# A linear layer with a low-rank update: semaphores of its own, a looped program for TensorE, and x rounded to bf16 ahead of the transposes

## Chip, core and metric

One core of one Trainium2 chip. The metric is the device time of one execution in microseconds. The core's engines are TensorE (PE; its weight loads are listed as PEld), VectorE (DVE), ScalarE (ACT), GpSimd (POOL) and SyncE (SP), and 16 DMA engines move data between DRAM and the on-chip memory SBUF. Matmuls write to a second on-chip memory, PSUM. The engines run their own instruction streams and wait for each other with semaphores.

## What is computed

```python
# x: (16, 2048, 256), W: (256, 256), lora_A: (256, 16), lora_B: (16, 256), lora_E: (16,)
x_flat = x.reshape(-1, in_dim)                  # 32768 rows of 256
y = x_flat @ W
lora_out = x_flat @ lora_A
lora_out = lora_out * lora_E
lora_out = lora_out @ lora_B
y = y + scale * lora_out
return y.reshape(batch, seq_len, out_dim).astype(np.float32)
```

x and the output are 33.5 MB each, in fp32.

## The kernel before

The low-rank update is folded into the weights once: `weff = W + (A * E * scale) @ B`, kept in bf16 (lines 87 to 105). Each row of x then meets one product, `x @ weff`.

x is worked through in nine chunks, `PLAN` on line 11: 16 rows of all 128 partitions (2 MB), seven times 32 rows (4 MB), and 16 again. A partition's rows are contiguous in DRAM, so a 4 MB chunk is one run of 32 KB per partition. Six buffers `xy` (`SLOTS`) hold chunks; the result is written over the chunk's own x, and stored from there.

All large transfers are issued by the sync engine on one queue, in this order: W; loads of chunks 0 to 3 (`LEAD`); then, for each chunk i, its store (line 70) and the load of chunk i + 4 (line 66). From chunk 6 on, a load first waits until the store that last used its buffer has landed. ScalarE's queue issues the three small loads.

Inside a chunk the work goes by groups of two rows (`CG`). For a group TensorE transposes four 128x128 blocks of x in fp32 against an identity (line 113) into a PSUM tile, VectorE copies them to SBUF as bf16 (line 119), TensorE multiplies with `weff` (line 131, four matmuls with 256 columns), and ScalarE copies the fp32 result from PSUM into the chunk's buffer (line 139). TensorE runs one group ahead: the transposes of group n + 1 come before the products of group n. There are 128 groups; every instruction of every engine is written out, with no loop in the program. The order is the one in which the kernel is written, and the framework (`tc.manual_schedule()`) places the semaphores and the waits.

Of the kernel before, what the change touches and what calls it, by code (L numbers as in the profile page):

```python
# [1 line left out]

# [5 lines left out]

PLAN = [16] + [32] * 7 + [16]

ROWS, SLOTS = 32, 6

LEAD = 4
CG = 2


@with_exitstack
def kernel(  # L20
    ctx: ExitStack,
    tc: tile.TileContext,
    x: bass.AP,
    W: bass.AP,
    lora_A: bass.AP,
    lora_B: bass.AP,
    lora_E: bass.AP,
    scale: bass.AP,
    out: bass.AP,
):  # L30
    nc = tc.nc
    P = 128
    FP32 = mybir.dt.float32
    BF16 = mybir.dt.bfloat16

    x_flat = x.flatten_outer_dims()
    out_flat = out.flatten_outer_dims()
    N, K = x_flat.shape
    M = out_flat.shape[1]
    R = lora_B.shape[0]  # L40
    KC = K // P
    assert K == M and sum(PLAN) * P == N

    const = ctx.enter_context(tc.tile_pool(name="const", bufs=1))
    slots = ctx.enter_context(tc.tile_pool(name="slots", bufs=SLOTS))
    xTpool = ctx.enter_context(tc.tile_pool(name="xTpool", bufs=4))
    ps_setup = ctx.enter_context(tc.tile_pool(name="ps_setup", bufs=1, space=bass.MemoryType.PSUM))
    ps_xT = ctx.enter_context(tc.tile_pool(name="ps_xT", bufs=3, space=bass.MemoryType.PSUM))
    ps_y = ctx.enter_context(tc.tile_pool(name="ps_y", bufs=3, space=bass.MemoryType.PSUM))


    ctx.enter_context(tc.manual_schedule())

    starts = [sum(PLAN[:i]) * P for i in range(len(PLAN))]

    def rows_of(flat, i):
        b, r0 = PLAN[i], starts[i]
        return flat[r0:r0 + b * P, :].rearrange("(p b) k -> p b k", b=b)

    held = []

    def load(i):
        t = slots.tile([P, ROWS, K], FP32, name="xy")
        nc.sync.dma_start(out=t[:, :PLAN[i], :], in_=rows_of(x_flat, i))  # L66
        held.append(t)

    def store(i):
        nc.sync.dma_start(out=rows_of(out_flat, i), in_=held[i][:, :PLAN[i], :])  # L70

    w_sb = const.tile([P, KC, M], FP32)
    nc.sync.dma_start(out=w_sb, in_=W.rearrange("(c p) m -> p c m", p=P))  # L73
    a_sb = const.tile([P, KC, R], FP32)
    nc.scalar.dma_start(out=a_sb, in_=lora_A.rearrange("(c p) r -> p c r", p=P))
    b_sb = const.tile([R, M], FP32)
    nc.scalar.dma_start(out=b_sb, in_=lora_B)
    e_sb = const.tile([R, 1], FP32)
    nc.scalar.dma_start(out=e_sb, in_=lora_E[:, None])

    for i in range(LEAD):
        load(i)

    ident = const.tile([P, P], FP32)
    make_identity(nc, ident)

    b_bf = const.tile([R, M], BF16)
    nc.vector.tensor_copy(out=b_bf, in_=b_sb)  # L88
    ps_at = ps_setup.tile([R, KC, P], FP32, name="ps_at")
    for c in range(KC):  # L90
        nc.tensor.transpose(ps_at[:, c, :], a_sb[:, c, :], ident)  # L91
    ate = const.tile([R, KC, P], BF16)
    nc.vector.tensor_scalar(  # L93
        out=ate,
        in0=ps_at,
        scalar1=e_sb,
        scalar2=float(scale),
        op0=mybir.AluOpType.mult,
        op1=mybir.AluOpType.mult,
    )  # L100
    ps_aeb = ps_setup.tile([P, KC, M], FP32, name="ps_aeb")
    for c in range(KC):
        nc.tensor.matmul(ps_aeb[:, c, :], ate[:, c, :], b_bf, start=True, stop=True)  # L103
    weff = const.tile([P, KC, M], BF16)
    nc.vector.tensor_add(out=weff, in0=w_sb, in1=ps_aeb)  # L105

    groups = [(i, g) for i, b in enumerate(PLAN) for g in range(b // CG)]

    def transposed(i, g):
        psum_xt = ps_xT.tile([P, CG, KC, P], FP32, name="psum_xt")  # L110
        for j in range(CG):
            for c in range(KC):
                nc.tensor.transpose(  # L113
                    psum_xt[:, j, c, :],
                    held[i][:, g * CG + j, c * P:(c + 1) * P],
                    ident,
                )
        xt = xTpool.tile([P, CG, KC, P], BF16, name="xt")
        nc.vector.tensor_copy(out=xt, in_=psum_xt)  # L119
        return xt  # L120


    ready = transposed(*groups[0])
    for n, (i, g) in enumerate(groups):
        xt = ready
        if n + 1 < len(groups):
            ready = transposed(*groups[n + 1])
        psum_y = ps_y.tile([P, CG, M], FP32, name="psum_y")
        for j in range(CG):
            for c in range(KC):  # L130
                nc.tensor.matmul(  # L131
                    psum_y[:, j, :],
                    xt[:, j, c, :],
                    weff[:, c, :],
                    start=(c == 0),
                    stop=(c == KC - 1),
                )

        nc.scalar.copy(out=held[i][:, g * CG:(g + 1) * CG, :], in_=psum_y)  # L139
        if (g + 1) * CG == PLAN[i]:  # L140
            store(i)
            if i + LEAD < len(PLAN):
                load(i + LEAD)


# [1 line left out]
_INS = ['x', 'W', 'lora_A', 'lora_B', 'lora_E', 'scale']  # L147
_OUTS = [((16, 2048, 256), 'float32')]

_NUMBERS = {'scale': 1.0}  # L150


# [26 lines left out]
```

## Time and profile before

| | |
|---|---|
| three runs | 165.45, 166.19, 166.29 us; median 166.19 |
| profiled execution | 166.25 us, span 164.4 us |
| TensorE busy (matmul) | 123.3 us, 1028 instructions |
| TensorE weight loads | 102.9 us, 1028 instructions |
| VectorE busy | 90.0 us, 131 instructions |
| ScalarE busy | 76.3 us, 129 instructions |
| DMA | 67.56 MB, mean 411 GB/s over the span |
| first load issued | 1.22 us after the span's start |
| ScalarE's last copy begins | 138.1 us |

The span runs from the first to the last instruction of the profiled execution. A row of a group in the profile is: line, engine, operation, output and inputs by the program's names, shapes, count; then busy time and the mean duration of one in ns; then the idle time of the engine just before them, with what ended it. In the slices each digit is the busy share, in tenths, of one fortieth of the span. A row of windows has the stretch, its length, the busy time of each engine with the number of instructions (PE, PEld, DVE, ACT, POOL), TensorE's granted clock, the DMA engines' share and GB/s. A row of the chain or of issues begins with the start and the duration in us. A row of waits has who waited for whom, the sum, the number of times and the longest.

### The profile page before, as it was taken

How to read it: one execution, taken by the hardware profiler on the slowest of the kernel's cores; microseconds unless marked ns; L12 is line 12 of the kernel's file. 1: busy time of each engine (PE TensorE's matmuls, PEld its weight loads, DVE VectorE, ACT ScalarE, POOL GpSimd, SP SyncE). 2: the span in 40 equal slices, each digit the busy share in tenths (PEclk: the TensorE clock that was granted, in tenths of full speed). 3: DMA queues.
4: the chain of work that ended last, by engine and by line, in shares of the span. 5: the costliest groups of instructions: out<-in, count | busy, mean ns of one | idle time of the engine just before them, and what ended most of it. 6: DMA issues, size and time to landing. Idle time of an engine off the chain costs nothing.

```text
span 164.4 us, 2548 instructions
## 1 busy us (share of the span) xinstructions
PE 123.3 (75%) x1028; PEld 102.9 (63%) x1028; DVE 90.0 (55%) x131; ACT 76.3 (46%) x129; POOL 0.7 (0%) x6
## 2 busy tenths in 40 slices
PE   0179899999999999999999689992999995000000
PEld 0058788888888888888888478881888783000000
DVE  0065677777777777777777536771777673000000
ACT  0034566666666666666666525662566565000000
POOL 1000000000000000000000000000000000000000
PEclk9999999999999999999999978999999999655555
DMA  5999999998999999999999999999999999999991
GB/s 141 429 482 407 415 478 395 454 415 343 437 462 407 421 446 431 435 431 423 439 419 439 423 423 443 409 439 447 423 391 466 415 443 423 423 454 415 415 391 56
DMA packets 3211, 67.56 MB, mean 411 GB/s; under 512 B 624, under 2 KB 896, under 8 KB 896
## 3 DMA queue, kind: packets, MB, share of 16 engines
q1 hardware_dynamic: 2864, 67.37, 96.2%
q8 instruction: 8, 0.13, 0.3%
q10 hardware_dynamic: 336, 0.03, 0.2%
q14 instruction: 3, 0.02, 0.0%
HBM read 33.85 MB, written 33.55 MB: 410 GB/s over the span
## 4 chain that ended last, share of the span: by engine, by line
DMA 59%; PE 23%; ACT 1%; SPq 1%; DVE 0%; issue 0%
DMA xy<-in_x_dram 38%; DMA out_dram<-xy 21%; PE psum_y L131 12%; PE psum_xt L113 11%; ACT xy L139 1%; DVE xt L119 0%; SPq L66 0%; SPq L73 0%
## 5 line engine op out<-in xcount | busy, mean ns | idle before, releaser
L119 DVE CAST xt<-psum_xt 128x512 bf16<-128x512 f32 x128 | 88.5, 691 | 38.6 <-PE psum_xt L113 38.6
L139 ACT COPY xy<-psum_y 128x512 f32<-128x512 f32 x128 | 75.0, 586 | 52.7 <-PE psum_y L131 52.7
L113 PE MATMUL psum_xt<-ident,xy 128*128 128x128 f32 x512 | 79.2, 279 | 6.1 <-DMA xy<-in_x_dram 6.0
L131 PE MATMUL psum_y<-weff,xt 128*128 128x256 bf16 x512 | 79.3, 278 | 0.3 <-DVE xt L119 0.3
L113 PEld LDWEIGHTS psum_xt<-ident,xy 128*128 128x128 f32 x512 | 61.9, 144 | 9.2 <-issue 5.7
L131 PEld LDWEIGHTS <-xt 128*128 128x128 bf16 x512 | 41.1, 99 | 16.8 <-DVE xt L119 0.9
L139 ACT ACT_TABLE_LOAD x1 | 1.3, 1283 | 9.7 <-DMA xy<-in_x_dram 9.7
L103 PE MATMUL ps_aeb<-b_bf,ate 16*128 16x256 bf16 x2 | 0.6, 402 | 4.4 <-DVE ate L93 4.4
L91 PE MATMUL ps_at<-ident,a_sb 128*16 128x128 f32 x2 | 0.6, 396 | 4.0 <-DMA a_sb<-in_lora_A_dram 4.0
L88 DVE CAST b_bf<-b_sb 16x256 bf16<-16x256 f32 x1 | 0.3, 281 | 6.0 <-DMA b_sb<-in_lora_B_dram 6.0
L103 PEld LDWEIGHTS <-ate 16*128 16x128 bf16 x2 | 0.1, 102 | 4.9 <-DVE ate L93 4.9
L91 PEld LDWEIGHTS ps_at<-ident,a_sb 128*16 128x16 f32 x2 | 0.1, 88 | 4.0 <-issue 4.0
L93 DVE TENSOR_SCALAR ate<-ps_at,e_sb 16x256 bf16<-16x256 f32 x1 | 0.5, 472 | 2.2 <-DMA e_sb<-in_lora_E_dram 2.2
L105 DVE TENSOR_TENSOR weff<-w_sb,ps_aeb 128x512 bf16<-128x512 f32 x1 | 0.7, 689 | 0.7 <-PE ps_aeb L103 0.7
masks.py:199 POOL TENSOR_SCALAR_AFFINE_SELECT ident<-ident 128x128 f32<-128x128 f32 x1 | 0.3, 292 | 0.1
masks.py:197 POOL MEMSET ident<- 128x128 f32 x1 | 0.2, 204 | 0.3 <-POOLq L160 0.3
L160 POOL MEMSET const-bfloat16-1.0<- 128x1 bf16 x1 | 0.1, 101 | 0.0
L160 POOL MEMSET const-uint8-127<- 128x1 uint8 x1 | 0.1, 101 | 0.0
L160 POOL MEMSET const-float32-0.0<- 128x1 f32 x1 | 0.1, 98 | 0.2 <-issue 0.2
L160 POOL MEMSET const-float32-1.0<- 128x1 f32 x1 | 0.1, 98 | 0.0
## 6 DMA issues: line engine op xcount, KB each, us to landing
xy<-in_x_dram SPq DMA_DIRECT2D x7, 4096.0 KB, 38.0
out_dram<-xy SPq DMA_DIRECT2D x7, 4096.0 KB, 34.2
xy<-in_x_dram SPq DMA_DIRECT2D x2, 2048.0 KB, 26.6
out_dram<-xy SPq DMA_DIRECT2D x2, 2048.0 KB, 24.5
w_sb<-in_W_dram SPq DMA_DIRECT2D x1, 256.0 KB, 3.0
a_sb<-in_lora_A_dram ACTq DMA_DIRECT2D x1, 16.0 KB, 3.2
b_sb<-in_lora_B_dram ACTq DMA_DIRECT2D x1, 16.0 KB, 4.7
e_sb<-in_lora_E_dram ACTq DMA_DIRECT2D x1, 0.1 KB, 6.6
```

The lines of the kernel that those rows point to most:

```text
L88: nc.vector.tensor_copy(out=b_bf, in_=b_sb)
L91: nc.tensor.transpose(ps_at[:, c, :], a_sb[:, c, :], ident)
L93: nc.vector.tensor_scalar(out=ate, in0=ps_at, scalar1=e_sb, scalar2=float(scale), op0=mybir.AluOpType.mult, op1=mybir.AluOpType.mult,)
L103: nc.tensor.matmul(ps_aeb[:, c, :], ate[:, c, :], b_bf, start=True, stop=True)
L105: nc.vector.tensor_add(out=weff, in0=w_sb, in1=ps_aeb)
L113: nc.tensor.transpose(psum_xt[:, j, c, :], held[i][:, g * CG + j, c * P:(c + 1) * P], ident,)
L119: nc.vector.tensor_copy(out=xt, in_=psum_xt)
L131: nc.tensor.matmul(psum_y[:, j, :], xt[:, j, c, :], weff[:, c, :], start=(c == 0), stop=(c == KC - 1),)
L139: nc.scalar.copy(out=held[i][:, g * CG:(g + 1) * CG, :], in_=psum_y)
L160: nc = _bacc.Bacc("TRN2", target_bir_lowering=False, num_devices=1)
```

## The change

The same arithmetic by other means, with every large transfer at the same place in the sync engine's program.

- The tile framework's pools are gone; buffers are allocated by hand. The whole kernel is one critical section of the framework (`tc.tile_critical`), with its own semaphores for loads, stores and each hand-over. The section is opened and closed by the sync engine: when it is entered the sync engine issues a token and every engine waits for it; at its end the sync engine waits for all stores and for tokens of all engines.
- The unit of work is a step of four rows (`Q`), 64 of them. VectorE rounds four rows of x to bf16 into one of two buffers `xb` (`round_step`), TensorE transposes eight blocks of bf16 into one of two bf16 PSUM tiles, VectorE copies these to one of two `xt`, TensorE runs eight products into one of two PSUM tiles, and ScalarE copies the result of four rows at once.
- TensorE's operands are now the same in every second step, so that its program is a loop of 31 iterations with two steps each. Its semaphores are counted down as they are taken (`take`), so that the waits in the loop are constants too. The other engines' programs are written out.
- ScalarE drains before it signals that a chunk is ready for its store.

The core of the diff:

```diff
-CG = 2
+Q = 4
...
-    ctx.enter_context(tc.manual_schedule())
+    xy = [sbuf(f"xy{s}", [P, ROWS, K], FP32) for s in range(SLOTS)]
+    xb = [sbuf(f"xb{s}", [P, Q, K], BF16) for s in range(2)]
+    xt = [sbuf(f"xt{s}", [P, Q, KC, P], BF16) for s in range(2)]
...
+    ps_xt = [psum(f"ps_xt{s}", [P, Q, KC, P], BF16) for s in range(2)]
+    ps_y = [psum(f"ps_y{s}", [P, Q, M], FP32) for s in range(2)]
...
+    with tc.tile_critical(sync_engine=mybir.EngineType.SP, no_gpsimd_drain=True):
...
+        sp.dma_start(out=w_sb[:], in_=W.rearrange("(c p) m -> p c m", p=P)).then_inc(s_w, 16)
+        for i in range(LEAD):
+            load(i)
+        for i in range(CHUNKS):
+            sp.wait_ge(s_rdy, i + 1)
+            sp.dma_start(out=rows_of(out_flat, i), in_=xy[i % SLOTS][:, :PLAN[i], :]).then_inc(s_out[i], 16)
+            if i + LEAD < CHUNKS:
+                if i + LEAD >= SLOTS:
+                    sp.wait_ge(s_out[i + LEAD - SLOTS], 16)
                 load(i + LEAD)
+        for i in range(CHUNKS):
+            sp.wait_ge(s_out[i], 16)
...
+        def round_step(k):
+            i, r = steps[k]
+            if r == 0:
+                dve.wait_ge(s_in[i], 16)
+            if k >= 2:
+                dve.wait_ge(s_t, k - 1)
+            dve.tensor_copy(out=xb[k % 2][:], in_=xy[i % SLOTS][:, r:r + Q, :]).then_inc(s_xb, 1)
+
+        round_step(0)
+        for k in range(n):
+            if k + 1 < n:
+                round_step(k + 1)
+            dve.wait_ge(s_t, k + 1)
+            if k >= 2:
+                dve.wait_ge(s_p, k - 1)
+            dve.tensor_copy(out=xt[k % 2][:], in_=ps_xt[k % 2][:]).then_inc(s_xt, 1)
...
+        for k, (i, r) in enumerate(steps):
+            act.wait_ge(s_p, k + 1)
+            act.copy(out=xy[i % SLOTS][:, r:r + Q, :], in_=ps_y[k % 2][:]).then_inc(s_y, 1)
+            if r + Q == PLAN[i]:
+                act.drain().then_inc(s_rdy, 1)
...
+        def take(s):
+            pe.wait_ge(s, 1).then_inc(s, -1)
+
+        def transposes(k):
+            take(s_xb)
+            for j in range(Q):
+                for c in range(KC):
+                    t = pe.transpose(ps_xt[k % 2][:, j, c, :], xb[k % 2][:, j, c * P:(c + 1) * P], ident_bf[:])
+            t.then_inc(s_t, 1)
+
+        def products(k):
+            take(s_xt)
+            take(s_y)
+            for j in range(Q):
+                for c in range(KC):
+                    m = pe.matmul(
+                        ps_y[k % 2][:, j, :], xt[k % 2][:, j, c, :], weff[:, c, :],
+                        start=(c == 0), stop=(c == KC - 1),
+                    )
+            m.then_inc(s_p, 1)
...
+        transposes(0)
+        pe.wait_ge(s_lora, 4)
+        with pe.Fori(0, n // 2 - 1):
+            transposes(1)
+            products(0)
+            transposes(0)
+            products(1)
+        transposes(1)
+        products(0)
+        products(1)
```

The setup has the same products and one more cast, of the identity to bf16 (`ident_bf`), on VectorE.

## The prediction

> **What bounds the kernel now.** I read the page's slices first, then the windows from 2 us to 160 us and from there to the end, the chain of waits, the sync engine's own issues, and the groups by line last.
>
> ```profile
> PE   0179899999999999999999689992999995000000
> DMA  5999999998999999999999999999999999999991
> 2.00:160.00 158.00, 123.29 (x1028) 102.91 (x1028) 89.95 (x131) 76.25 (x129) 0.00 (x0) 0.93 1.00 426
> 160.00:164.40 4.40, 0.00 (x0) 0.00 (x0) 0.00 (x0) 0.00 (x0) 0.00 (x0) 0.50 0.14 60
> q1 hardware_dynamic: 2864, 67.37, 96.2%
> q8 instruction: 8, 0.13, 0.3%
> ```
>
> The 16 DMA engines have a share of 1.00 over 158 us, at 426 GB/s; 158 x 426 = 67.3 MB, which is all that the kernel moves. TensorE is done at slice 34 of 40 and the DMA goes on without it. Queue q8 is no data: eight packets that fetch instructions.
>
> ```profile
> 1.72 17.63 DMA xy<-in_x_dram
> 50.54 34.17 DMA out_dram<-xy
> 84.77 44.76 DMA xy<-in_x_dram
> 138.10 0.58 ACT xy L139
> ...
> 96.98 42.06 SPq L70 DMA_DIRECT2D out_dram<-xy  x4
> ...
> out_dram<-xy SPq DMA_DIRECT2D x2, 2048.0 KB, 24.5
> ```
>
> In the chain a 4 MB load that is issued at 84.77 lands 44.76 us later, though 4.19 MB at 426 GB/s is 9.8 us: the queue holds some 35 us of work ahead of it. The last result is written at 138.68, its 2 MB store is issued at 138.7, and it lands 24.4 us later, at 163.1; the work of its own is 4.9 us. So compute has slack, and the time is the bytes by the rate, plus 2 us of start and what stands behind the last landing. The span is 164.4, the profiled execution 166.25 (1.85 lie around the span); the median of the runs is 166.19, 0.06 lower.
>
> **How much slack.** A step is 4 rows of all 128 partitions; there are 64, eight in a large chunk and four in the first and last. Today TensorE sets its pace: four matmuls of a group take 0.44 to 0.52 us in the chain, a step has four such groups, 1.92 us. Let a step take p. Chunk 1 lands at 19.4 and everything behind it can run without a wait. With 2 us from the last product to the store's issue, chunk 7's store goes out at 21.3 + 56p. If the queue has run dry by then, 9.9 us for this store, 4.9 for the last and 2.4 of fixed latency follow (the 0.26 MB load of W, 0.6 us of bytes, took 3.0). 21.3 + 56p + 17.2 = 163.1 gives p = 2.22. The same sum for chunk 6 gives 2.4. Up to 2.2 us a step, compute moves nothing; the order in which the sync queue issues loads and stores, and the landing that each late load waits for (six slots), are the same in both programs.
>
> **The change part by part.**
>
> ```profile
> L119 DVE CAST xt<-psum_xt 128x512 bf16<-128x512 f32 x128 | 88.5, 691 | 38.6 <-PE psum_xt L113 38.6
> L139 ACT COPY xy<-psum_y 128x512 f32<-128x512 f32 x128 | 75.0, 586 | 52.7 <-PE psum_y L131 52.7
> L113 PE MATMUL psum_xt<-ident,xy 128*128 128x128 f32 x512 | 79.2, 279 | 6.1 <-DMA xy<-in_x_dram 6.0
> L131 PE MATMUL psum_y<-weff,xt 128*128 128x256 bf16 x512 | 79.3, 278 | 0.3 <-DVE xt L119 0.3
> L88 DVE CAST b_bf<-b_sb 16x256 bf16<-16x256 f32 x1 | 0.3, 281 | 6.0 <-DMA b_sb<-in_lora_B_dram 6.0
> SPq L160 <- PEq L160: 0.7, 1, 0.7
> SPq L174 <- PEq L174: 0.6, 2, 0.4
> ```
>
> *VectorE.* Added: 64 roundings of 1024 elements, SBUF to SBUF. The nearest row is the cast of 256 at line 88, 281 ns. [...] Moved: 128 copies of 512 become 64 of 1024, from bf16 in PSUM. [...] A step is 0.69 + 1.23 = 1.92, with two waits some 2.0 (1.4 to 2.5).
>
> [...]
>
> *ScalarE.* 64 copies of 1024: the 586 ns are 427 at 1.2 elements a ns and 159 fixed, so 0.85 + 0.16 = 1.01 us, and a drain a chunk; below VectorE.
>
> *TensorE.* Eight products keep 0.88 to 1.04 a step. Eight transposes of bf16 cost between a half and all of today's 0.88. Three semaphores are taken a step and a branch closes every two: 1.3 to 2.0 with 0.1 for these, and I take 1.6. VectorE is the slowest at 2.0, so compute ends a few us later than now, under 20 us of stores: nothing. If that cover went, each 0.1 us in a step would cost 56 x 0.1 = 5.6 us.
>
> *Start.* The section opens with a token from the sync engine that all wait for, ahead of W's load and the first load. Today's opening wait of this kind is 0.7 us, the two of line 174 0.3 each. The sync engine gives the token itself: +0.2 (0 to 0.7), and all of it is on the path, since every byte starts later. The other edits of the setup (one more cast, the identity in bf16) end before the first load lands or sit in the slack.
>
> *End.* After the last landing the sync engine passes nine waits, eight of them long met, then waits for all engines' tokens and gives one, before the closing that exists now: +0.3 (0 to 0.7, the same rows).
>
> *Instruction fetch.* TensorE's 2056 recorded instructions become a loop of some 70 with its waits. q8's 131 KB by 2056 is 64 bytes each, so q8 is this program; the eight packets go. Each holds one DMA engine for 0.3% x 16 x 164.4 / 8 = 1.0 us, and the trace has the data packet behind it late by some 0.45 more. As a mean over 16 engines that is 8 x 1.0 / 16 = 0.5; on the engine that ends last between 0 and 1.4. I take -0.5.
>
> *Semaphores of its own.* The waits of the loads and stores stand at the same places. Nothing.
>
> Sum on 166.25: +0.2 +0.3 -0.5 = 0, less the 0.06 to the median: 166.2 us. With all bounds 164.8 to 167.6.
>
> **The rivals.** *The fetches were worth more.* The last DMA engine ends over 1 us behind the next by the trace's packets, and if fetches made it the last, their full 1.4 goes and the tokens cost nothing: 166.2 - 1.4 = 164.8. For it: a packet of q8 lies in the last 30 us, when nothing evens it out. Against: data packets also show stretches in which one engine is some 5% slow, with no fetch near.
>
> *The tokens at their upper bounds*, with the fetches worth nothing: 166.2 + 1.4 = 167.6. For it: the opening wait of 0.7. Against: the two of 0.3.
>
> [...]
>
> *The loop does not hold its program* (slower, and the change would not do what it says): each of 31 backward branches waits for a packet of 16 KB, 1.0 us and the 2.4 of latency, 1.7 us a step on TensorE: p = 1.6 + 1.7 = 3.3, 21.3 + 56 x 3.3 + 17.2 = 223, and 226 in time. Against: two steps are well under the 256 instructions of one fetched packet. [...]
>
> **How the numbers follow.** What a measurement here can tell from no change is about 0.5%, 0.83 us. The forecast, within that of 166.2: 0.64. More from the fetches: 0.15. Tokens dear: 0.10. VectorE bound: 0.07. Refetching loop: 0.04. So faster 0.15, same 0.64, slower 0.21. The range runs from 164.9 to 167.7: it takes in the bounds of the tokens and fetches and leaves out the two compute cases, 0.11 together, and a little at the low end.
>
> **What would show it.** In the changed profile: DMA share still 1.00 from 2 us to 160 and 426 GB/s; q8 gone; the first load issued at 1.2 to 1.9; the rounding near 690 ns and the copy at 691 or 1225; ScalarE's last copy between 130 and 145 us, well before the last landing at 163; 1.3 to 2.0 from there to the end of the span. I am wrong if the DMA's slices fall under 9 ahead of the end, if the chain has VectorE or TensorE in its last 30 us, or if the rate of the full stretch is another than 426.

## The result and the profile after

| | before | after |
|---|---|---|
| 16 runs each | 166.14 us (165.45 to 166.64) | 167.18 us (166.42 to 167.74) |
| profiled execution | 166.25 us, span 164.4 | 166.75 us, span 165.0 |
| 27 and 10 runs on another occasion | 166.00 us | 166.85 us |

The changed kernel takes 1.0066 of the time before (95% interval 1.0054 to 1.0079), and 1.0047 (1.0030 to 1.0063) the second time: slower by some 0.8 to 1.0 us, about the 0.5% that was called the limit of what can be told. The forecast was 166.2 with a range from 164.9 to 167.7.

The page of the changed kernel, slices and groups:

```profile
PE   0159499999996599408994099902998591000000
DMA  5999998997999999999999999999999999999970
...
q1 hardware_dynamic: 2864, 67.37, 95.7%
...
q14 instruction: 3, 0.02, 0.0%
...
L160 ACT COPY xy<-ps_y 128x1024 f32<-128x1024 f32 x64 | 64.8, 1012 | 69.2 <-PE ps_y L181 69.2
L181 PE MATMUL ps_y<-weff,xt 128*128 128x256 bf16 x512 | 72.1, 288 | 0.8 <-PEq L167 0.3
L173 PE MATMUL ps_xt<-ident_bf,xb 128*128 128x128 bf16 x512 | 43.6, 235 | 30.4 <-PEq L167 30.4
L143 DVE CAST xb<-xy 128x1024 bf16<-128x1024 f32 x64 | 43.7, 684 | 32.9 <-DMA xy<-in_x_dram 32.9
L152 DVE COPY xt<-ps_xt 128x1024 bf16<-128x1024 bf16 x64 | 44.2, 690 | 10.2 <-PE ps_xt L173 9.1
```

TensorE now has holes of whole slices (VectorE waits 32.9 us in all for loads, TensorE 30.4 us ahead of its transposes), and the DMA is as full as it was: 1.00 and 426 GB/s from 2 us to 160. Queue q8, the fetches of TensorE's program, is gone from the list. A rounding takes 684 ns; the copy from PSUM has twice the elements of the old one and takes the same 690 ns. Behind a landed load the timeline has a step every 1.32 us, with TensorE back to back:

```profile
61.09 0.61 PE L173 MATMUL ps_xt<-ident_bf,xb 128*128 128x128 bf16 x8
...
62.41 0.61 PE L173 MATMUL ps_xt<-ident_bf,xb 128*128 128x128 bf16 x8
```

In the kernel before, the chain has 16 such steps from 20.12 to 49.45, 1.83 us each.

The two ends of the kernel before, first from the timeline of the sync engine (start and duration in us):

```profile
0.74 0.42 SPq L73 DMA_DIRECT2D w_sb<-in_W_dram  x1
1.22 1.90 SPq L66 DMA_DIRECT2D xy<-in_x_dram  x4
```

and then from the view of its closing line (least, median and largest duration in ns, first and last start in us):

```profile
L174 POOLq EVENT_SEMAPHORE_RANGE_CLEAR  x1: 96/96/96, 164.0 to 164.0; - x1
```

The same timeline of the changed kernel:

```profile
0.94 0.44 SPq L101 DMA_DIRECT2D w_sb<-in_W_dram  x1
1.44 1.89 SPq L99 DMA_DIRECT2D xy<-in_x_dram  x4
```

the view of the line that opens and closes its section:

```profile
L94 SPq NOP  x2: 13/13/13, 0.7 to 164.0; - x2
```

and that of its last line:

```profile
L237 POOLq EVENT_SEMAPHORE_RANGE_CLEAR  x1: 243/243/243, 164.4 to 164.4; - x1
```

The first load is issued 0.22 us later: the section's token stands before it (the first NOP, at 0.7), and after it a branch of every engine into the section (at 0.8). At the end the trace's semaphore events put the last wait for a store at 163.46 before and 163.48 after; from there to the span's end it is 0.94 us before and 1.49 after. Of the 0.55 more, 0.37 lie in the section's closing, a branch and the tokens (the second NOP, at 164.0, stands ahead of the framework's own closing), and 0.18 mostly in the clearing of the semaphores, 243 ns for 96. So 0.77 us are fixed costs at the two ends. The last store lands at the same time as before, though it started later: 163.08 against 163.11. In this pair of profiles, then, at most some 0.25 us were gained on the way.

Where the gain from the missing fetches went is seen in windows over the last 6 us (length; busy time by engine; TensorE's clock, the DMA share and GB/s last), before, after, and for the changed kernel with the loop written out (e7 below):

```profile
158.00:160.00 2.00, 0.00 (x0) 0.00 (x0) 0.00 (x0) 0.00 (x0) 0.00 (x0) 0.50 0.96 410
160.00:162.00 2.00, 0.00 (x0) 0.00 (x0) 0.00 (x0) 0.00 (x0) 0.00 (x0) 0.50 0.29 123
162.00:164.00 2.00, 0.00 (x0) 0.00 (x0) 0.00 (x0) 0.00 (x0) 0.00 (x0) 0.50 0.02 8
```

```profile
158.00:160.00 2.00, 0.00 (x0) 0.00 (x0) 0.00 (x0) 0.00 (x0) 0.00 (x0) 0.50 0.77 328
160.00:162.00 2.00, 0.00 (x0) 0.00 (x0) 0.00 (x0) 0.00 (x0) 0.00 (x0) 0.50 0.17 74
162.00:164.00 2.00, 0.00 (x0) 0.00 (x0) 0.00 (x0) 0.00 (x0) 0.00 (x0) 0.50 0.02 8
```

```profile
158.00:160.00 2.00, 0.00 (x0) 0.00 (x0) 0.00 (x0) 0.00 (x0) 0.00 (x0) 0.50 0.86 369
160.00:162.00 2.00, 0.00 (x0) 0.00 (x0) 0.00 (x0) 0.00 (x0) 0.00 (x0) 0.50 0.35 147
```

The share falls earlier after the change (0.77 and 0.17 for 0.96 and 0.29): most of the 16 engines are done sooner. From 162 to 164 us it is 0.02 both times (8 GB/s, one packet of 16 KB), and that packet belongs to the engine that ends last. The end is this engine's, and in this pair it did not move.

### The profile page after: what moved, and what is told of

Its sections match the earlier page's. It is cut to its first block, busy times and chain, and to the rows that moved or that the text cites. A ratio compares the mean times of both kernels' runs of the same rounds, so it can differ in the third digit from the quotient of the medians.

```text
span 165.0 us, 2679 instructions
## 1 busy us (share of the span) xinstructions
PE 97.6 (59%) x1028; PEld 85.6 (52%) x1028; DVE 84.0 (51%) x132; ACT 66.1 (40%) x65; POOL 0.7 (0%) x6
## 5 line engine op out<-in xcount | busy, mean ns | idle before, releaser
L160 ACT COPY xy<-ps_y 128x1024 f32<-128x1024 f32 x64 | 64.8, 1012 | 69.2 <-PE ps_y L181 69.2
L181 PE MATMUL ps_y<-weff,xt 128*128 128x256 bf16 x512 | 72.1, 288 | 0.8 <-PEq L167 0.3
L173 PE MATMUL ps_xt<-ident_bf,xb 128*128 128x128 bf16 x512 | 43.6, 235 | 30.4 <-PEq L167 30.4
L143 DVE CAST xb<-xy 128x1024 bf16<-128x1024 f32 x64 | 43.7, 684 | 32.9 <-DMA xy<-in_x_dram 32.9
L173 PEld LDWEIGHTS ps_xt<-ident_bf,xb 128*128 128x128 bf16 x512 | 37.7, 106 | 34.2 <-issue 32.4
L181 PEld LDWEIGHTS ps_y<-weff,xt 128*128 128x128 bf16 x512 | 50.2, 103 | 8.1 <-issue 1.7
L152 DVE COPY xt<-ps_xt 128x1024 bf16<-128x1024 bf16 x64 | 44.2, 690 | 10.2 <-PE ps_xt L173 9.1
```

The lines of the kernel that those rows point to most:

```text
L143: dve.tensor_copy(out=xb[k % 2][:], in_=xy[i % SLOTS][:, r:r + Q, :]).then_inc(s_xb, 1)
L152: dve.tensor_copy(out=xt[k % 2][:], in_=ps_xt[k % 2][:]).then_inc(s_xt, 1)
L160: act.copy(out=xy[i % SLOTS][:, r:r + Q, :], in_=ps_y[k % 2][:]).then_inc(s_y, 1)
L173: t = pe.transpose(ps_xt[k % 2][:, j, c, :], xb[k % 2][:, j, c * P:(c + 1) * P], ident_bf[:])
L181: m = pe.matmul(ps_y[k % 2][:, j, :], xt[k % 2][:, j, c, :], weff[:, c, :], start=(c == 0), stop=(c == KC - 1),)
```

## The experiments

**e1, e7: the loop written out.** Only TensorE's program changes; eight 16 KB fetches come back.

```diff
-        with pe.Fori(0, n // 2 - 1):
+        for _ in range(n // 2 - 1):
```

> The changed kernel with TensorE's loop written out, so that its program is fetched by some eight 16 KB packets again; all else is the same. The last landing moved from 163.11 to 163.08 us in the two profiles, though the first load started 0.2 later. Theory A (the end is set by the one DMA engine that is late, and the fetches are worth nothing there): the ratio to the kernel before stays at 1.0066 within 0.002, about 167.2 us. Theory B (the fetches are worth the 0.5 that was forecast, up to 0.8): 1.0096 to 1.0115, about 167.7 to 168.0 us. Either way the mean landing of the last store over the 16 engines goes from 160.2 back to some 160.9.

Measured: 167.16 us, ratio 1.0049 (1.0032 to 1.0066). So the looped program is not faster. That was measured beside the kernel before, not beside the changed one, so both were run on one chip:

> The changed kernel once more, on the same chip as the next run. Both theories: 1.0054 to 1.0079 of the kernel before.

> The changed kernel with TensorE's loop written out, now beside the changed kernel on one chip. The first time it took 1.0049 (1.0032 to 1.0066), so eight fetches more cost nothing that shows; the mean landing of the last store was 161.19 against 160.17, the last one 163.76 against 163.08. Theory A (the late DMA engine sets the end, and the fetches seldom fall on it): within 0.3 us of the changed kernel in the median. Theory B (the fetches are worth 0.5 to 0.8): 0.5 to 0.8 us over it.

Measured: the changed kernel 166.85 us, ratio 1.0047 (1.0030 to 1.0063); with the loop written out 166.75 us, 1.0039 (1.0022 to 1.0057). In time theory A holds: eight fetches more cost nothing that shows, and the 0.5 us of theory B lie outside the scatter of these runs. The two steps of a pass through the loop take no longer for its branch either: written out, a step also takes 1.32 us. The ends of the last store's packets, by DMA engine, in the profiles:

| profile | fetches in q8 | mean end of 16 engines, us | last engine, us |
|---|---|---|---|
| before | 8 | 160.78 | 163.11 |
| e1, loop written out | 8 | 161.19 | 163.76 |
| e7, loop written out | 8 | 160.67 | 162.57 |
| after | 0 | 160.17 | 163.08 |
| e6, after once more | 0 | 160.01 | 163.16 |
| e2, block version | 0 | 160.13 | 163.00 |

Without fetches the mean is 0.5 to 1.2 us earlier, about what the forecast's eight times 1.0 to 1.45 us over 16 engines say (0.5 to 0.7); the last engine is 2.9 to 3.2 us behind the mean without them and 1.9 to 2.6 with them. This fits the reading that the fetches fill time that most engines have over. It is not shown engine by engine: the trace's packets do not name their engine, and which engines the eight fetches fell on cannot be told from them without doubt. With fetches the last end also scatters over 1.2 us (162.57 to 163.76), so the ends alone would not decide; the times of e6 and e7 do.

**e2: no section.** The same programs and semaphores in a plain block, without the framework's context, with one closing barrier and one clearing.

```diff
-    with tc.tile_critical(sync_engine=mybir.EngineType.SP, no_gpsimd_drain=True):
+    with nc.Block(no_gpsimd_drain=True) as block:
...
+    nc.all_engine_barrier(sems_to_clear=range(min(h.num for h in sems), max(h.num for h in sems) + 1))
```

> The changed kernel without the framework's section and context: the same programs and semaphores in a plain block, with one closing barrier and one clearing of the semaphores. No opening token, no closing token. Theory A (the opening and closing cost 0.2 + 0.55 us by the two profiles): first load issued at 1.22 instead of 1.44, 0.9 to 1.2 us instead of 1.5 from the end of the last wait for a store to the end of the span, together 0.5 to 0.8 less, ratio 1.002 to 1.0036, about 166.4 to 166.7 us. Theory C (the added rounding on VectorE disturbs the transfers, and the tokens are hidden): ratio stays over 1.005.

Measured: 166.63 us, ratio 1.0015 (0.9997 to 1.0033), a little under the expected interval. The first load is issued at 1.23:

```profile
1.23 2.19 SPq L102 DMA_DIRECT2D xy<-in_x_dram  x4
```

Between the last wait and the span's end lie 1.07 us instead of 1.49. So 0.63 us of the ends are gone in the profile, and the ratio falls by 0.0032 to 0.0051, 0.5 to 0.8 us. Rounding, bf16 transposes, four-row steps and the loop are all still in it, and together they cost nothing that these runs can tell. Theory C falls.

**e3: W's load out of the sync engine's queue.** What stands ahead of the first load seemed to be on the path, so W went to ScalarE's queue, behind the three small loads.

```diff
-        sp.dma_start(out=w_sb[:], in_=W.rearrange("(c p) m -> p c m", p=P)).then_inc(s_w, 16)
...
         act.dma_start(out=e_sb[:], in_=lora_E[:, None]).then_inc(s_e, 16)
+        act.dma_start(out=w_sb[:], in_=W.rearrange("(c p) m -> p c m", p=P)).then_inc(s_w, 16)
```

> The changed kernel with W's load moved from the head of the sync engine's queue to the end of ScalarE's three small loads. Theory A (every byte of x waits for the start, so what stands ahead of the first load is on the path): the first load is issued at 0.94 instead of 1.44, the time falls by 0.3 to 0.5 us, ratio 1.0036 to 1.0048. Rival (W's bytes take their share of the engines wherever they stand, and only the issue is moved): under 0.1 us, ratio 1.006 to 1.0066.

Measured: 181.44 us, ratio 1.0900 (1.0876 to 1.0924). Neither theory had this. The landing times of the loads (KB each, us to landing):

```profile
w_sb<-in_W_dram ACTq DMA_DIRECT2D x1, 256.0 KB, 36.6
a_sb<-in_lora_A_dram ACTq DMA_DIRECT2D x1, 16.0 KB, 17.6
```

and two windows of the same run (columns as above: length, PE, weight load, DVE, ACT and POOL busy, clock, DMA share, GB/s):

```profile
2.00:33.00 31.00, 1.20 (x4) 0.23 (x4) 0.75 (x2) 1.28 (x1) 0.00 (x0) 1.00 1.01 421
36.00:46.00 10.00, 5.38 (x40) 4.50 (x41) 5.15 (x9) 1.01 (x1) 0.00 (x0) 1.00 0.14 59
```

lora_A takes 17.6 us instead of 3.1, W 36.6 instead of 2.9. `weff` is ready near 40 us, the four first loads are through by then, no store is ready, and the DMA stands nearly idle for 10 us (share 0.14). In the trace lora_A has 256 runs of 64 bytes, 16 for each engine, and from 4 us on these come one per engine every 0.61 us, the time of a 16 KB packet of chunk 0, and behind chunk 0 every 1.21 us, that of a 32 KB packet; the last of them ends at 16.8 us: one run to each packet of the large loads. Issued ahead of the large loads, the same runs went through in under 1 us (2.6 to 3.5 us in the changed kernel). W's place at the head, 0.5 us ahead of chunk 0, had kept the large loads back until lora_A was nearly through: in the changed kernel W's packets run from 2.03 to 3.48 us, and the first packet of chunk 0, which is issued at 1.44, begins at 3.15.

**e5, e11: how much compute is free.** Each rounding is issued three times (e5) or twice (e11) into the same buffer; the output is unchanged.

```diff
+            for e in range(EXTRA):
+                dve.tensor_copy(out=xb[k % 2][:], in_=xy[i % SLOTS][:, r:r + Q, :]).then_inc(s_spare, 1)
+                dve.wait_ge(s_spare, k * EXTRA + e + 1)
             dve.tensor_copy(out=xb[k % 2][:], in_=xy[i % SLOTS][:, r:r + Q, :]).then_inc(s_xb, 1)
```

> The changed kernel with each rounding on VectorE issued three times into the same buffer, each extra one waited for; the result is the same. VectorE then needs 3 x 0.684 + 0.690 = 2.74 us a step and some 2.9 with the waits, over the 2.22 from which the forecast has compute decide. The forecast's sum gives the last landing at 21.3 + 56 x 2.9 + 17.2 = 201 us and a time of 204. Rival (the queue holds more work than that sum says): under 185 us.

> The changed kernel with each rounding issued twice. With three the step took 2.655 us and the last landing came at 189.4, where the forecast's sum gives 187 for that pace. With two I expect 0.70 less, 1.95 us a step, under the 2.22 from which compute decides. Theory (compute has 0.2 us a step left): ratio as the changed kernel, 1.004 to 1.008, last landing 162.5 to 163.5. Rival (the longer steps delay loads and so drain the queue): over 1.012.

Measured: e5 193.0 us (one run), last landing 189.4, under the 204 and 201 that were expected and over the rival's 185. e11 166.58 us, ratio 1.0036 (1.0016 to 1.0055), last landing 162.97. The timeline of VectorE in e5 (start, duration; neighbours of one kind are drawn together):

```profile
59.64 1.41 DVE L146 CAST xb<-xy 128x1024 bf16<-128x1024 f32 x2
61.09 0.69 DVE L148 CAST xb<-xy 128x1024 bf16<-128x1024 f32 x1
61.70 0.68 DVE L157 COPY xt<-ps_xt 128x1024 bf16<-128x1024 bf16 x1
62.30 1.41 DVE L146 CAST xb<-xy 128x1024 bf16<-128x1024 f32 x2
```

and two windows of e5:

```profile
2.00:110.00 108.00, 62.70 (x593) 44.40 (x594) 98.96 (x154) 37.72 (x37) 0.00 (x0) 1.00 1.01 429
110.00:160.00 50.00, 30.90 (x302) 21.99 (x299) 48.69 (x77) 18.87 (x19) 0.00 (x0) 1.00 0.66 276
```

A step takes 62.30 - 59.64 = 2.66 us, not the 2.9 that was expected, since instructions in a row overlap a little (the rounding that starts at 61.09 takes 0.69, and the copy behind it starts at 61.70). With 2.655 the forecast's sum gives 21.3 + 56 x 2.655 + 17.2 = 187.2 for the last landing, 2.2 short of 189.4. The windows show the mechanism: for 110 us the queue's store of work hides the slow compute (share 1.01), then it is used up (0.66). In e11 a step takes 1.93 us, 46% longer than the 1.32 of the changed kernel, and nothing is lost. The point from which compute decides lies between 1.93 and 2.66.

**e8, e9: both ends cut.** From the block version: chunk 0 first, then the small loads and W on the same queue behind it, so that one queue carries all loads; and GpSimd clears the semaphores behind the block's one barrier. e9 also has 23 semaphores for 31 and one last wait for nine (the expectations count 22 and 34; the programs have 23 and 31).

```diff
-            sp.dma_start(out=w_sb[:], in_=W.rearrange("(c p) m -> p c m", p=P)).then_inc(s_w, 16)
-            for i in range(LEAD):
+            load(0)
+            sp.dma_start(out=a_sb[:], in_=lora_A.rearrange("(c p) r -> p c r", p=P)).then_inc(s_a, 16)
...
+            sp.dma_start(out=w_sb[:], in_=W.rearrange("(c p) m -> p c m", p=P)).then_inc(s_w, 16)
+            for i in range(1, LEAD):
                 load(i)
...
-    nc.all_engine_barrier(sems_to_clear=range(min(h.num for h in sems), max(h.num for h in sems) + 1))
+    nc.gpsimd.sem_clear(range(min(h.num for h in sems), max(h.num for h in sems) + 1))
```

> The block version with two more things taken off both ends: the sync engine issues chunk 0 first, then the three small loads and W on the same queue behind it, then chunks 1 to 3; and after the block's one barrier GpSimd clears the semaphores with no second barrier. Theory A (only what stands at the two ends counts, and compute may start some 7 us later for nothing): first load issued at 0.74 instead of 1.22, worth 0.3 to 0.5; 0.75 instead of 1.0 us from the last store's wait to the end; together 0.5 to 0.8 under the block version's 1.0015, so 0.9965 to 0.9985, about 165.6 to 165.9 us. Rival (the later setup or the small loads behind a large one cost more, as when W went to ScalarE's queue): 1.002 and above.

> The lean version with 22 semaphores instead of 34 (loads of the same buffer share one, the last six stores share one), and one wait for the last stores instead of nine. The clearing took 96 ns in the kernel before, 243 in the changed one and 203 in the block and lean versions: some 6 ns a semaphore. Theory A: clearing some 140 ns, 0.05 to 0.15 us less in time than the lean version's 0.9994, so 0.9985 to 0.999, which these rounds hardly tell apart; the closing in the profile does. Rival: no change in the closing.

Measured: e8 165.90 us, 0.9994 (0.9977 to 1.0011); e9 165.81 us, 0.9993 (0.9978 to 1.0009). The timeline of the sync engine in e8:

```profile
0.74 0.38 SPq L102 DMA_DIRECT2D xy<-in_x_dram  x1
1.18 0.42 SPq L105 DMA_DIRECT2D a_sb<-in_lora_A_dram  x1
...
2.65 0.42 SPq L108 DMA_DIRECT2D w_sb<-in_W_dram  x1
3.12 1.50 SPq L102 DMA_DIRECT2D xy<-in_x_dram  x3
```

Against the changed kernel that is 0.5 to 0.7% less, as large as the changed kernel's whole loss; against the kernel before neither is distinguishable. Chunk 0 goes out 0.49 us earlier than in the block version, but the mean end of the engines comes only 0.2 us earlier (159.92) and the last one 0.07 (162.93). The queue's first transfer is issued at 0.74 in both, W in the block version and chunk 0 in e8, and the bytes of both have to be moved. e8's gain over the block version is 0.0021 in the ratio, 0.35 us, where 0.5 to 0.8 were expected; the closing alone, 0.69 us from the last wait to the span's end instead of 1.07, accounts for it. Of e9's edit the profile shows the clearing at 160 ns instead of 203, not the 140 that was expected (6 ns for each of the 8 semaphores that are gone makes 155); the time does not show it.

**e10, e12: the late engine.** Two attempts, both from e9, at the 3 us by which one engine ends behind the mean.

```diff
+                to, by = rows_of(out_flat, i), xy[i % SLOTS][:, :PLAN[i], :]
+                if i == CHUNKS - 1:
+                    sp.dma_start(out=to[:120], in_=by[:120]).then_inc(s_rest, 16)
+                    sp.dma_start(out=to[120:], in_=by[120:]).then_inc(s_rest, 16)
...
```

> The same with the last store split in two: partitions 0 to 119 in one, which I expect on 15 of the DMA engines, and the last 8 in another, on 8 of those. In all profiles with a full queue the last engine ends 1.9 to 3.2 us behind the mean of the 16, and two or three engines are late. If a fixed engine outside the 15 is the late one, it ends 4.9 us earlier and the end is set by the second late one: last landing 0.4 to 0.7 us earlier, ratio 0.995 to 0.997. If the late one is among the 15, nothing or up to 0.6 us later: 0.9985 to 1.003.

Measured: 169.45 us, ratio 1.0209 (1.0182 to 1.0236), outside both expectations. Of the 128 packets of the last store 35 take over 1.0 us instead of 0.61, but these do not set the end. The engine that ends last (166.67) moves its packets of the last store at 0.61 us each; it comes to them only at 161.19, because two 32 KB packets of the store before took 3.58 and 2.19 us instead of 1.21, 3.3 us in all, while the others already moved the last store. Why they did is open. This engine moves one more packet after its share of the 120, so it is one of the eight that carry the last 8 partitions, and from 130 to 137 us, in the store of chunk 5, its packets took 1.25 to 1.32 us: it was late before the split as well.

```diff
-        return flat[r0:r0 + b * P, :].rearrange("(p b) k -> p b k", b=b)
+        return flat[r0:r0 + b * P, :].rearrange("(h p b) k -> p h (b k)", p=P, b=16)
```

> The lean version with 22 semaphores, and the 4 MB chunks moved as two runs of 16 KB per partition from two places of the chunk, where all others move one run of 32 KB; bytes, engines and order are the same. In the full-queue profiles the late engine falls behind in the loads, with packets of 1274 to 1330 ns where the others take 1213. If that hangs on the addresses or the length of a run, the last landing comes within 1.5 us of the mean of the 16 engines instead of 2.8 to 3.2, and the ratio falls to 0.990 to 0.994. If it hangs on the engine, the last landing stays 2.5 us or more behind the mean, ratio 0.998 to 1.002.

Measured: 166.10 us, ratio 1.0002 (0.9983 to 1.0022), last landing 162.71, 2.4 us behind the mean of 160.28. The ratio is the one expected if the lateness hangs on the engine, the distance falls just short of its bound. So the lateness does not seem to hang on the addresses and the length of the runs, as far as one profile can say; why an engine falls behind stays open. The packets of 1274 to 1330 ns, which the expectation places in the loads, are packets of stores: in the changed kernel such a stretch lies between 53 and 62 us, in the store of chunk 1, whose landing releases the load that is issued at 64.01.

## Why the forecast held, and what was wrong in it

*What bounds the kernel* was right. The rate of the full stretch is 426 GB/s from 2 to 160 us in both kernels, and e11 (1.93 us a step, nothing lost) and e5 (2.66, 26 us lost) stand on either side of the forecast's 2.22 us a step. The 1.92 us for the step of the kernel before is too high; the chain has 1.83, and nothing in the sum hangs on it. Two of the signs named for being wrong did come, and they were badly chosen: the changed kernel has a DMA slice of 7 and TensorE in the chain at 135.6 us, within the last 30, but the kernel before has a slice of 8 and TensorE in the chain at 137.5 as well.

*VectorE*: no run shows the paces behind the 0.69 and the 1.23 in the forecast's step; the runs showed 0.684 for a rounding, which 0.69 had right, and 0.690 for the copy from PSUM, for which 1.23 was too dear. A bf16 copy of 1024 elements takes the time of an fp32 copy of 512 (0.691), twice its pace, which no row of the kernel before showed. The step is TensorE's, 1.32 us and not 2.0, which changes nothing in the time. *ScalarE*: 1.01 was right: 512 elements took 586 ns and 1024 take 1012, which is 1.2 elements a ns and 160 ns fixed.

*Start*: +0.2, measured +0.22 at the first issue. That all of it is on the path is not shown by itself: the last landing came no later in the one pair of profiles (163.08 for 163.11), and 0.2 us are too little to tell in the times. *End*: +0.3, measured +0.55. The right mechanism, mis-sized: the section's closing costs 0.37 of it, and the clearing of more semaphores, 0.15, was not in the sum; "Semaphores of its own" was put at nothing by the waits alone. Both ends together count: with 0.63 us of them taken off (e2) the time falls by 0.5 to 0.8.

*Instruction fetch*: "I take -0.5" is the step that failed. The packets were real and so was their price (0.91 to 1.07 us for each of the eight in the kernel before), as the means of the DMA engines' ends show (160.17 for 160.78), but the sum took that mean for the end, and the end is the last engine's. The bound named beside it ("on the engine that ends last between 0 and 1.4") had the answer at its lower end: e7 beside the changed kernel is 0.1 us faster, not 0.5 slower.

With these two terms as measured the sum is 166.25 + 0.22 + 0.55 + 0 - 0.06 = 166.96 us, between the two medians of 167.18 and 166.85. The range held, by its bounds on tokens and fetches; its middle was 0.65 to 1.0 us too low. The outcome with the largest chance, within 0.5% (0.83 us) of the kernel before, came only at its edge: 1.04 us over in the first measurement, 0.85 in the second. Closest is the rival with dear tokens, in kind if not in full: tokens at 0.6 rather than 1.4, and the fetches worth nothing. The rival in which the fetches are worth more did not come, nor did the two of compute: 684 and 690 ns excluded VectorE as the bound, and the loop's branch back shows no wait of microseconds: two steps take 2.64 us, branch included.

## What to carry to other kernels

Where the DMA is full from end to end and compute has slack, as here (share 1.00 from 2 us to 160), work that was moved or made cheaper inside counted for nothing (a step of 1.32 us instead of 1.83 saved no time, and one of 1.93 in e11 cost none), and half a microsecond of tokens, barriers and semaphore clearing at the two ends showed in the time (0.63 us in e2 were worth 0.5 to 0.8); those can be read off the issue of the first transfer and the stretch behind the last landing. A saving that is spread over 16 DMA engines should be priced at the engine that ends last, not at the mean (here the mean end came 0.61 us earlier, the last 0.03). Before moving a small load to another queue, ask what large loads it will then share the engines with (in e3 lora_A took 17.6 us instead of 3.1, and the kernel 1.09 of the time).

## What the runs showed of the hardware

- A load of 16 KB in runs of 64 bytes, issued 0.04 us ahead of megabytes on another queue, took 17.6 us (e3); issued 0.53 us ahead, 3.1 (the changed kernel). In e8, issued behind chunk 0 on one queue, all its runs moved between 7.3 and 8.2 us.
- With a full queue some DMA engines end 2 to 3 us after the mean. Followed by their times, each packet beginning where one ended, the late ones are of two kinds. One engine is slow in the stores of chunks 1 to 5, with over twenty 32 KB packets of 1250 to 1350 ns where the others take 1213; it ends last in e11 (162.97), but second to last in the changed kernel (162.39). The engine that ends last there (163.08) has normal packets but for single ones, most of them loads, of up to 1.8 us.
- With compute as the bound (e5, share 0.66 from 110 us to 160) the queue empties between transfers, and the 16 engines end within 0.17 us.
- A store over 120 partitions instead of 128 (e10) had 35 of 128 packets over 1.0 us instead of 0.61.
- Clearing the semaphores at the end took 203 ns for 31 of them (e2, e8) and 160 ns for 23 (e9).
